# HGRN2's level and state products in a two-layer hybrid encoder: from 128-column products to 64-column blocks on the two halves of the PE array

## The chip, the cores and the metric

One Trainium2 chip; the kernel runs on one of its cores. The metric is device time in microseconds of one execution. An engine executes its own queue in order; TensorE is called PE, VectorE DVE, ScalarE ACT, GpSimdE POOL, the sync engine's queue SP. Weight loads of PE stand under a name of their own, PEld.

## The reference

Two encoder layers over 512 tokens of width 1024. Each layer projects x with one large matrix, feeds three token mixers (HGRN2, dilated attention, latent attention), merges them through gates, projects, and normalizes. The change touches only HGRN2: a gated linear recurrence for 8 heads, key width 128, value width 64, run forward and backward in time:

```
S_t = diag(f_t) S_{t-1} + k_t v_t^T ;  o_t = S_t^T q_t
```

Everything is float32.

## The kernel before

Tokens lie along the free axis, 512 of them in 4 blocks of 128; one tile of 128 partitions holds the 128 key channels of one head. Projections with the large matrices split both operands into a high and a low part and run three passes of single-pass products (lines 291 to 316); they make up most of PE's stream: hq and hf (queries and gates of a head), hv and dv (values), hgg, dl, mg and so on.

`hgrn_levels` (line 686) works for one head as a generator. The recurrence is split in a doubling scheme. In every level m = 1, 2, 4, 8, 16, 32, 64 the running products of gates are folded into qq and kk in place by two DVE multiplications (lines 738, 739). At m = 4 (lines 697 to 721) both directions of the innermost 8-token triangles are made: for each direction, key and query tiles hk and hq are put together from a part that ACT copies (line 707) and a part that POOL multiplies (line 709), four products of 128 x 128 per direction go to PE (line 716), ACT copies the bank to `ha` or `hz` (line 717), POOL clears what lies on the wrong side of the diagonal (line 719), and DVE adds the two (line 721). At m = 8, 16, 32, 64 (lines 722 to 733) ACT gathers the keys kc (line 726), PE makes four products of 128 x 128, one per block of tokens (line 729), and DVE copies under a mask those elements of the product that belong to the level into `ha` (line 733). Each level thus computes all 128 x 128 pairs of a block, and the mask keeps the few that it is for.

After the levels the kk tiles are transposed on PE (line 754), copied by ACT (line 756), and six products of 128 weight columns with 64 moving columns give the block states `hst` (line 762), which DVE chains (lines 766 to 775). `hgrn_pair` (line 779) adds up the outputs of two heads in one bank, the first head on partitions 0 to 63, the second on 64 to 127: products with 64 weight columns, on alternating halves of the array (line 796). `do` (line 975) and `dn` (line 1019) in the dilated attention have that form as well; two of the `do` products per head pair and half move 64 columns only.

Heads go in pairs (lines 1065 to 1075). The two generators of a pair are stepped in turn until both give their result. Then the projections of the next pair are traced (hq, hf) and, for the first two pairs, a value projection of the dilated attention (dv); the first pair's run beside the value projection hv. The engines' queues aren't in the order of tracing: a scheduler at build time, with durations of its own, lays the traced instructions out, earlier-traced first among those it holds ready, so that projections of the next pair lie between the levels of the current one. Buffers bound this: three PSUM banks for such products (`at_bank`), four for projections, 16 tiles of 128 x 512 with tag a2 (hk, hq, kc, ha, hz and others), 6 and 4 large tiles for gates, kk and qq. `after(first, *before)` (line 232) adds a dependency by hand: the instruction `first` waits for those in `before`.

Of the kernel before, what the change touches and what calls it, by code (L numbers as in the profile page):

```python
# [11 lines left out]
I32 = mybir.dt.int32  # L12
# [29 lines left out]

HG_LEVELS = (8, 16, 32, 64)
PI = float(np.pi)


# [14 lines left out]
def host_tables():  # L61

    i = np.arange(128)
    masks = np.zeros((128, len(HG_LEVELS), 128), np.int32)
    for n, m in enumerate(HG_LEVELS):
        a, b = i[:, None], i[None, :]
        masks[:, n, :] = (a // (2 * m) == b // (2 * m)) & (a // m != b // m)
    ident = np.eye(128, dtype=np.float32)
# [129 lines left out]
def tile_encoder(ctx: ExitStack, tc: tile.TileContext, x, xt, positions, blocks, wuq, wuh, par_in, brow, lbp,  # L198
# [40 lines left out]
    con = cst.tile([128, N_CONST], F32, name="con")  # L239
    mask = cst.tile([128, len(HG_LEVELS) * 128], U8, name="mask")  # L240
    ident = con[:, O_ID:O_ID + 128]
# [209 lines left out]
    nc.sync.dma_start(con, consts)  # L451
    mask_i = fap(t4("mask_i", I32), 0, [[1, len(HG_LEVELS) * 128]])
    nc.sync.dma_start(mask_i, masks)
    V.tensor_copy(mask, mask_i)

    def layer(l, x_src, need_next):
# [229 lines left out]
        def hgrn_levels(h, g, v):  # L686
# [9 lines left out]
            while m < 128:  # L696
                if m == 4:

                    rc = fap(f2, 0, [[1, 2 * R]])
                    V.reciprocal(rc, fap(base, 0, [[1, 2 * R]]))  # L700
                    a, z = t2(f"ha{h}_{l}"), t2(f"hz{h}_{l}")
                    for d, dst in ((0, a), (1, z)):
                        kd, qd = t2(f"hk{d}{h}_{l}"), t2(f"hq{d}{h}_{l}")

                        for t, src, plain in ((kd, kk[:, d], m * d), (qd, qq[:, 1 - d], m - m * d)):
                            scaled = m - plain
                            A.copy(fap(t, plain, [[2 * m, R // 2], [1, m]]),  # L707
                                   fap(src, plain, [[2 * m, R // 2], [1, m]]))
                            nc.gpsimd.tensor_tensor(
                                fap(t, scaled, [[2 * m, R // 2], [1, m]]),  # L710
                                fap(src, scaled, [[2 * m, R // 2], [1, m]]),
                                fap(rc, R * (1 - d) + scaled // m, [[2, R // 2], [0, m]]), ALU.mult)
                        sc = at_bank(f"hs{h}_{d}_{l}")
                        for w in range(NT):
                            ws = slice(w * 128, w * 128 + 128)
                            nc.tensor.matmul(sc[:, ws], kd[:, ws], qd[:, ws], start=True, stop=True)  # L716
                        A.copy(dst, sc)  # L717
                        sgn = 1 - 2 * d
                        nc.gpsimd.affine_select(dst, dst, pattern=[[0, NT], [sgn, 128]], compare_op=ALU.is_ge,  # L719
                                                fill=0.0, base=0, channel_multiplier=-sgn)  # L720
                    V.tensor_tensor(a, a, z, ALU.add)
                elif m > 4:

                    sc = at_bank(f"hs{h}_{m}_{l}")
                    kc = t2(f"kc{h}_{m}_{l}")
                    A.copy(fap(kc, 0, [[2 * m, R // 2], [m, 2], [1, m]]),  # L726
                           fap(kk, 0, [[2 * m, R // 2], [S + m, 2], [1, m]]))
                    for w in range(NT):
                        nc.tensor.matmul(sc[:, w * 128:w * 128 + 128], kc[:, w * 128:w * 128 + 128],  # L729
                                         fap(qq, w * 128, [[2 * m, 64 // m], [S + m, 2], [1, m]]),  # L730
                                         start=True, stop=True)
                    n = HG_LEVELS.index(m)
                    ready = [V.copy_predicated(a, bcast(mask[:, n * 128:n * 128 + 128], [[0, 4], [1, 128]]), sc)]  # L733

# [16 lines left out]
            for d, blocks in ((0, (0, 1, 2)), (1, (1, 2, 3))):  # L751
                tr = at_bank(f"hkt{h}{d}_{l}")
                for j, b in enumerate(blocks):
                    nc.tensor.transpose(tr[:, j * 128:j * 128 + 128], kk[:, d, b * 128:b * 128 + 128], ident)  # L754
                kt_ = t2(f"hkt{h}{d}_{l}")
                A.copy(kt_[:, :384], tr[:, :384])  # L756
# [487 lines left out]
```

## Time and profile before

| | us |
|---|---|
| median of 3 runs | 1806.01 (1804.51 to 1806.61) |
| profiled execution | 1804.81 |
| its span in the trace | 1803.1 |
| PE busy in the span | 1776.1 |
| DVE, ACT, POOL busy | 1051.9, 743.5, 569.4 |

The span runs from the first to the last instruction; the execution's own time is 1.7 us more. A busy PE is not PE at its peak, because its records overlap: the time that a group of records takes is read from the start of the first to the start of what follows, not from the sum of durations. A float32 product appears as two MATMUL and two LDWEIGHTS records. In the names of the groups "128*64 128x128" means 128 rows and 64 columns of weights, and 128 partitions by 128 moving columns.

### The profile page before, as it was taken

To read this page: it belongs to the slowest core of one execution; us is meant where nothing else is said; L and a number is where in the kernel's file an instruction comes from. 1 tells how busy PE (TensorE), PEld (TensorE's weight loads), DVE (VectorE), ACT (ScalarE), POOL (GpSimd) and SP (SyncE) were. 2 spreads that over 40 slices of the span, in tenths; PEclk is the share of its full clock that TensorE was granted. 3 is DMA by queue.
4 is the path that set the end of the run, shared out by engine and by line. 5 is a ranking of instruction groups with operands and counts; after the bars stand their busy time and mean duration, and the time that the engine had idled before them with its cause. 6 is when DMAs were issued, how large, how long until landed. Compare 5 with 4: busy or idle time off the path is not lost.

```text
span 1803.1 us, 24561 instructions
## 1 busy us (share of the span) xinstructions
PE 1776.1 (99%) x9656; PEld 1499.6 (83%) x9656; DVE 1051.9 (58%) x1870; ACT 743.5 (41%) x1291; POOL 569.4 (32%) x306
## 2 busy tenths in 40 slices
PE   9999999999999999999999999999999999999987
PEld 7788988988888888887788889889888888888876
DVE  8887766543232466656576767775432324656565
ACT  6545454233334364433254345442424244544330
POOL 0311245134243233333222112542333332433332
PEclk9999999999999999999999999999999999999999
DMA  5212222122222222322242122222222232224222
GB/s 191 89 58 101 70 72 86 59 83 82 71 94 83 68 74 78 119 101 70 94 134 97 62 88 72 70 88 66 64 94 83 71 95 57 90 73 148 76 68 79
DMA packets 77139, 154.10 MB, mean 85 GB/s; under 512 B 37728, under 2 KB 37728, under 8 KB 77024
## 3 DMA queue, kind: packets, MB, share of 16 engines
q1 hardware_dynamic: 77024, 152.54, 26.4%
q8 instruction: 76, 1.25, 0.3%
q14 instruction: 39, 0.32, 0.1%
HBM read 148.22 MB, written 4.29 MB: 85 GB/s over the span
## 4 chain that ended last, share of the span: by engine, by line
PE 93%; DVE 4%; ACT 1%; issue 0%; POOL 0%; DMA 0%; SPq 0%; DVEq 0%
PE mg L297 17%; PE dl L297 15%; PE dv L314 8%; PE hf L297 7%; PE br L297 6%; PE wo L1189 4%; PE hq L297 4%; PE hs L729 3%; PE hgg L297 2%; PE dg L297 2%; PE hv L314 2%; PE st L495 2%; PE cq L297 2%; PE do L975 2%; PE mo L656 2%; PE hs L716 1%
## 5 line engine op out<-in xcount | busy, mean ns | idle before, releaser
L690 POOL TENSOR_TENSOR qq<-hq,fr 128x1024 f32<-128x1024 f32 x16 | 41.9, 2622 | 249.5 <-DVE fr L683 249.5
L739 DVE TENSOR_TENSOR kk<-kk,fr 128x512 f32<-128x512 f32 x96 | 89.1, 946 | 23.6 <-ACT hk L707 16.3
L1035 DVE TENSOR_SCALAR mg<-mg 128x512 f32<-128x512 f32 x32 | 53.6, 1682 | 55.3 <-ACT mg L1034 55.1
L738 DVE TENSOR_TENSOR qq<-qq,fr 128x512 f32<-128x512 f32 x96 | 73.4, 764 | 0.0
L733 DVE COPY_PREDICATED ha<-mask,hs 128x512 f32<-128x512 uint8 x64 | 46.9, 733 | 43.9 <-PE hs L729 43.9
L729 PEld LDWEIGHTS hs<-qq,kc 128*128 128x128 f32 x512 | 62.6, 192 | 2.9 <-ACT kc L726 0.6
L729 PE MATMUL hs<-qq,kc 128*128 128x128 f32 x512 | 63.1, 275 | 0.4 <-DVE qq L738 0.4
L854 DVE CUSTOM_DVE_ANT_0 zb<-dsb,con 128x256 f32<-128x256 f32 x64 | 23.3, 421 | 51.9 <-PE dsb L907 51.9
L726 ACT COPY kc<-kk 128x512 f32<-128x512 f32 x64 | 38.5, 623 | 35.0 <-DVE kk L739 34.9
L756 ACT COPY hkt<-hkt 128x384 f32<-128x384 f32 x32 | 15.0, 507 | 87.7 <-PE hkt L754 87.7
L652 ACT COPY mpt<-mtr 128x128 f32<-128x128 f32 x64 | 17.0, 266 | 77.2 <-DVE mpt L652 77.2
L272 POOL TENSOR_TENSOR wb_0l<-wb_0r,wb_0h 128x1024 fp32r<-128x1024 f32 x12 | 29.3, 2445 | 58.2 <-ACT wb_0h L271 47.2
L272 POOL TENSOR_TENSOR wb_1l<-wb_1r,wb_1h 128x1024 fp32r<-128x1024 f32 x12 | 29.4, 2448 | 56.6 <-ACT wb_1h L271 45.5
L837 DVE TENSOR_SCALAR dl<-dl,par,con 128x512 f32<-128x512 f32 x24 | 25.9, 1080 | 35.1 <-PE dl L297 35.1
L955 ACT ACTIVATE za<-za,dst 128x256 f32<-128x256 f32 x64 | 30.0, 470 | 29.7 <-DVE dst L949 29.7
L652 DVE COPY mpt<-mtr 128x128 f32<-128x128 f32 x64 | 18.5, 288 | 39.9 <-PE mtr L650 32.0
L1035 DVE TENSOR_SCALAR mgc<-mgc 128x512 f32<-128x512 f32 x16 | 24.7, 1546 | 24.3 <-ACT mgc L1034 24.3
L719 POOL TENSOR_SCALAR_AFFINE_SELECT ha<-ha 128x512 f32<-128x512 f32 x16 | 10.3, 645 | 87.5 <-ACT ha L717 61.1
L716 PEld LDWEIGHTS hs<-hq,hk 128*128 128x128 f32 x256 | 33.2, 191 | 4.2 <-issue 2.0
L647 DVE TENSOR_SCALAR mp<-mp,mst 128x512 f32<-128x512 f32 x32 | 35.6, 1111 | 0.9
L716 PE MATMUL hs<-hq,hk 128*128 128x128 f32 x256 | 34.0, 276 | 1.3 <-POOL ha L719 1.3
L656 PE MATMUL mo<-mpt,mv 128*128 128x128 f32 (+1 forms) x192 | 33.5, 309 | 0.0
(1511 smaller groups left out, 5437.8 us busy)
## 6 DMA issues: line engine op xcount, KB each, us to landing
wb_0r<-in_blocks_dram SPq DMA_DIRECT2D x12, 512.0 KB, 3.5
wb_1r<-in_blocks_dram SPq DMA_DIRECT2D x12, 512.0 KB, 3.5
w_0r<-in_blocks_dram SPq DMA_DIRECT2D x9, 512.0 KB, 3.5
w_1r<-in_blocks_dram SPq DMA_DIRECT2D x8, 512.0 KB, 3.5
w_2r<-in_blocks_dram SPq DMA_DIRECT2D x8, 512.0 KB, 3.4
w_3r<-in_blocks_dram SPq DMA_DIRECT2D x8, 512.0 KB, 3.4
wo_0r<-in_blocks_dram SPq DMA_DIRECT2D x8, 512.0 KB, 3.5
wo_1r<-in_blocks_dram SPq DMA_DIRECT2D x8, 512.0 KB, 3.4
```

The source lines that it names most:

```text
L272: (eng or nc.gpsimd).tensor_tensor(lo, raw, hi.bitcast(F32), ALU.subtract)
L297: newest["product"] = nc.tensor.matmul(ps, lhs(a, k), rhs(b, k), start=n == 0, stop=n == 3 * kt - 1)
L314: nc.tensor.matmul(ps, xs[a][2 * j + k][:, toks], w[b][:, k], start=j == 0 and n == 0, stop=j == 3 and n == 5)
L656: nc.tensor.matmul(o[:, cols], v[:, kb, h * 128:h * 128 + 128], pts[kb][:, cols], start=qt == 1 and kb == 0, stop=qt == NT - 1 and kb == N ...
L690: nc.gpsimd.tensor_tensor(qq, bcast(q, [[0, 2], [1, S]]), fr, ALU.mult)
L716: nc.tensor.matmul(sc[:, ws], kd[:, ws], qd[:, ws], start=True, stop=True)
L729: nc.tensor.matmul(sc[:, w * 128:w * 128 + 128], kc[:, w * 128:w * 128 + 128], fap(qq, w * 128, [[2 * m, 64 // m], [S + m, 2], [1, m]]), s ...
L733: ready = [V.copy_predicated(a, bcast(mask[:, n * 128:n * 128 + 128], [[0, 4], [1, 128]]), sc)]
L738: V.tensor_tensor(fap(qq, 0, dims), fap(qq, 0, dims), qf, ALU.mult)
L739: V.tensor_tensor(fap(kk, 0, dims), fap(kk, 0, dims), kf, ALU.mult)
L1035: V.tensor_scalar(g, g, 0.5, 0.5, ALU.mult, ALU.add)
L1189: nc.tensor.matmul(ps, ms[a][2 * kp + k][:, tt * 128:tt * 128 + 128], wo[4 * half + kp][b][k][:, cols], start=(kp, a, b, k) == (0, 0, 0, 0 ...
```

## The change

- The level products at m = 4, 8, 16 and 32 are made for the 64 x 64 blocks on the diagonal only: eight products with 64 weight columns and 64 moving columns, alternately onto partitions 0 to 63 and 64 to 127 of the bank, in place of four of 128 x 128. At m = 64 the eight products are the blocks beside the diagonal.
- At m = 4 both directions share one bank; ACT copies it once (to a new tile `hc`), and four half-width selects on POOL take the place of two.
- Levels 32 and 64 write into one bank, each its own blocks, and share one masked copy after level 64. Levels 8 and 16 have two masked copies, each of 64 partitions and 64 columns of each block.
- The state products go as 64-column halves too: twelve products with 64 weight columns in place of six with 128.
- The generators hand their products out as functions; the loop over pairs calls those of both heads one after the other and makes the first of them wait for the inputs of both heads.
- The table of masks has three entries in place of four.

```diff
-HG_LEVELS = (8, 16, 32, 64)
+HG_MASKS = ((8,), (16,), (32, 64))
+HALVES = [(slice(64 * i, 64 * i + 64), slice(c + 64 * i, c + 64 * i + 64)) for c in range(0, S, 128) for i in range(2)]
...
                     a, z = t2(f"ha{h}_{l}"), t2(f"hz{h}_{l}")
-                    for d, dst in ((0, a), (1, z)):
+                    kds, qds, made = [], [], []
+                    for d in range(2):
                         kd, qd = t2(f"hk{d}{h}_{l}"), t2(f"hq{d}{h}_{l}")
...
-                        sc = at_bank(f"hs{h}_{d}_{l}")
-                        for w in range(NT):
-                            ws = slice(w * 128, w * 128 + 128)
-                            nc.tensor.matmul(sc[:, ws], kd[:, ws], qd[:, ws], start=True, stop=True)
-                        A.copy(dst, sc)
+                    sc, c = at_bank(f"hs{h}_{l}"), t2(f"hc{h}_{l}")
+                    first = None
+                    for d in range(2):
+                        for n, (rows, at) in enumerate(HALVES):
+                            mat = nc.tensor.matmul(sc[rows, 256 * d + 64 * (n // 2):256 * d + 64 * (n // 2) + 64],
+                                                   kds[d][:, at], qds[d][:, at], start=True, stop=True)
+                            first = first or mat
+                    after(first, *made)
+                    A.copy(c, sc)
+
+                    for d, dst in ((0, a), (1, z)):
                         sgn = 1 - 2 * d
-                        nc.gpsimd.affine_select(dst, dst, pattern=[[0, NT], [sgn, 128]], compare_op=ALU.is_ge,
-                                                fill=0.0, base=0, channel_multiplier=-sgn)
+                        for i in range(2):
+                            nc.gpsimd.affine_select(fap(dst, 64 * i, [[128, NT], [1, 64]]),
+                                                    fap(c, 256 * d, [[64, NT], [1, 64]]),
+                                                    pattern=[[0, NT], [sgn, 64]], compare_op=ALU.is_ge, fill=0.0,
+                                                    base=64 * i * sgn, channel_multiplier=-sgn)
                     V.tensor_tensor(a, a, z, ALU.add)
                 elif m > 4:
-                    sc = at_bank(f"hs{h}_{m}_{l}")
+                    if m < 64:
+                        sc = at_bank(f"hs{h}_{m}_{l}")
                     kc = t2(f"kc{h}_{m}_{l}")
...
+                    def products(m=m, sc=sc, kc=kc):
+                        first = None
+                        for n, (rows, at) in enumerate(HALVES):
+                            if m < 64:
+                                to, rhs = at, fap(qq, at.start, [[2 * m, 32 // m], [S + m, 2], [1, m]])
+                            else:
+                                c = at.start + 64 * (1 - 2 * (n % 2))
+                                to = slice(c, c + 64)
+                                rhs = qq[:, 1 - n % 2, to]
+                            mat = nc.tensor.matmul(sc[rows, to], kc[:, at], rhs, start=True, stop=True)
+                            first = first or mat
+                        return first
+
+                    yield [made], products
+                    if m != 32:
+                        n = [m in ms for ms in HG_MASKS].index(True)
+                        for cols in [slice(0, 128)] if m == 64 else [slice(0, 64), slice(64, 128)]:
+                            rows, wd = slice(0, 128) if m == 64 else cols, cols.stop - cols.start
+                            mk = mask[rows, n * 128 + cols.start:n * 128 + cols.stop]
+                            ready = [V.copy_predicated(fap(a[rows], cols.start, [[128, NT], [1, wd]]),
+                                                       bcast(mk, [[0, NT], [1, wd]]),
+                                                       fap(sc[rows], cols.start, [[128, NT], [1, wd]]))]
...
-            yield
-            n = 0
-            for d, blocks in ((0, (0, 1, 2)), (1, (1, 2, 3))):
-                for j, b in enumerate(blocks):
-                    nc.tensor.matmul(st[:, n * 64:n * 64 + 64], kts[d][:, j * 128:j * 128 + 128],
-                                     v[:, b, 64 * h:64 * h + 64], start=n == 0, stop=n == 5, skip_group_check=True)
-                    n += 1
+            def states():
+                first, n = None, 0
+                for d, blocks in ((0, (0, 1, 2)), (1, (1, 2, 3))):
+                    for j, b in enumerate(blocks):
+                        for i in range(2):
+                            c = j * 128 + 64 * i
+                            mat = nc.tensor.matmul(st[64 * i:64 * i + 64, n * 64:n * 64 + 64], kts[d][:, c:c + 64],
+                                                   v[:, b, 64 * h:64 * h + 64], start=n == 0, stop=n == 5,
+                                                   skip_group_check=True)
+                            first = first or mat
+                        n += 1
+                return first
+
+            yield [made], states
...
-            parts = [None]
-            while None in parts:
+            while True:
                 parts = [next(g) for g in both]
+                if parts[0] is None:
+                    continue
+                if len(parts[0]) > 2:
+                    break
+
+                firsts = [go() for _, go in parts]
+                after(firsts[0], *parts[0][0], *parts[1][0])
```

At level 4 the wait is for the inputs of the head itself (`after(first, *made)`), at the later levels and the states for those of both heads.

## Rows read from the trace of the kernel before

**Rows 1.** The page: busy time, share of the span and instructions of each engine; PE's granted clock in 40 slices, in tenths of full speed; the chain that ended last by engine.

```profile
PE 1776.1 (99%) x9656; PEld 1499.6 (83%) x9656; DVE 1051.9 (58%) x1870; ACT 743.5 (41%) x1291; POOL 569.4 (32%) x306
...
PEclk9999999999999999999999999999999999999999
...
PE 93%; DVE 4%; ACT 1%; issue 0%; POOL 0%; DMA 0%; SPq 0%; DVEq 0%
```

**Rows 2.** Busy time by stage, from the first pair's level products in layer 0 on: stretch and its length, then busy us (and records) of PE, PEld, DVE, ACT and POOL, granted clock, DMA share and GB/s.

```profile
62.00:92.00 30.00, 27.28 (x135) 22.68 (x134) 21.04 (x28) 23.95 (x35) 7.69 (x9) 1.00 0.30 100
...
138.00:211.00 73.00, 73.00 (x412) 66.53 (x411) 55.24 (x84) 33.85 (x54) 14.76 (x14) 1.00 0.23 76
```

**Rows 3.** What PE waited for over the whole run: who waited for whom, us in total, times, longest us.

```profile
PE hq L297 <- DVE hv L511: 1.4, 1, 1.4
...
PE hs L716 <- POOL ha L719: 1.3, 1, 1.3
...
PE hs L729 <- DVE qq L738: 0.4, 1, 0.4
```

**Rows 4.** Groups of PE instructions by line and shape: busy us and mean ns of one, then idle time before them.

```profile
L729 PE MATMUL hs<-qq,kc 128*128 128x128 f32 x512 | 63.1, 275 | 0.4 <-DVE qq L738 0.4
L716 PE MATMUL hs<-hq,hk 128*128 128x128 f32 x256 | 34.0, 276 | 1.3 <-POOL ha L719 1.3
L762 PE MATMUL hst<-hv,hkt 128*128 128x64 f32 x192 | 23.7, 276 | 0.0
```

**Rows 5.** PE in order of time: start and duration in us, then line, operation, names, shape and count. Level products inside the projection stream, second pair of layer 0.

```profile
163.28 1.98 PE L297 MATMUL hf<-xh,w_1664h 128*128 128x512 f32 x8
165.09 1.95 PE L729 MATMUL hs<-qq,kc 128*128 128x128 f32 x16
166.79 2.07 PE L297 MATMUL hf<-xl,w_1664h 128*128 128x512 f32 x8
168.71 1.98 PE L297 MATMUL hf<-xh,w_1664l 128*128 128x512 f32 x8
170.52 1.98 PE L297 MATMUL hf<-xh,w_2688h 128*128 128x512 f32 x8
...
180.11 1.95 PE L729 MATMUL hs<-qq,kc 128*128 128x128 f32 x16
```

**Rows 6.** The same view where the dilated attention's products run on the two halves of the array, 64 weight columns and 128 moving columns, between two stretches of the stream.

```profile
656.84 0.39 PE L609 MATMUL mvps<-mvw0l,ckvn 128*128 128x512 f32 x1
657.16 1.09 PE L975 MATMUL do<-dtb30p,dv 128*64 128x128 f32 x16
658.08 1.04 PE L975 MATMUL do<-dtb31p,dv 128*64 128x128 f32 x16
658.95 1.04 PE L1019 MATMUL dn<-con,dden 128*64 128x128 f32 x16
659.93 0.50 PE L609 MATMUL mvps<-mvw0l,ckvn 128*128 128x512 f32 x1
660.26 0.86 PE L609 MATMUL mvps<-mvw0h,ckvn 128*128 128x512 f32 x3
```

**Rows 7.** The same view at a place where the last 8 records of such a run move 64 columns (the shape printed for a merged group is that of its first record).

```profile
434.79 1.09 PE L975 MATMUL do<-dta00p,dv 128*64 128x128 f32 x16
435.71 0.84 PE L975 MATMUL do<-dta01p,dv 128*64 128x128 f32 x16
436.48 0.66 PE L986 MATMUL dtb<-con,zb 128*128 128x128 f32 x4
```

**Rows 8.** The instructions of that line: durations in ns as minimum, median and maximum, first and last start, and the shapes, both layers together.

```profile
L975 PE MATMUL do<-dta01p,dv x32: 219/248/273, 435.7 to 1330.3; 128*64 128x128 f32 x16, 128*64 128x64 f32 x16
```

**Rows 9.** PE in order of time around the output products of a pair: 40 records on the halves between 203.06 and 205.39.

```profile
202.50 0.63 PE L314 MATMUL dv<-w_2l,xh 128*128 128x512 f32 x2
203.06 0.44 PE L796 MATMUL ho<-ha,hv 128*64 128x128 f32 x4
...
205.39 0.87 PE L314 MATMUL dv<-w_3h,xh 128*128 128x512 f32 x2
206.10 0.40 PE L314 MATMUL dv<-w_3h,xl 128*128 128x512 f32 x1
```

**Rows 10.** POOL in order of time at the level-4 stage of the third pair; in brackets its idle time before, and what ended it.

```profile
201.41 1.13 POOL L709 TENSOR_TENSOR hq<-qq,f 128x256 f32<-128x256 f32 x1
...
213.61 0.67 POOL L709 TENSOR_TENSOR hk<-kk,f 128x256 f32<-128x256 f32 x1
...
219.58 0.64 POOL L719 TENSOR_SCALAR_AFFINE_SELECT hz<-hz 128x512 f32<-128x512 f32 x1 [4.67 <-ACT hz L717]
220.19 0.67 POOL L709 TENSOR_TENSOR hk<-kk,f 128x256 f32<-128x256 f32 x1
220.81 1.12 POOL L709 TENSOR_TENSOR hq<-qq,f 128x256 f32<-128x256 f32 x1
```

**Rows 11.** DVE in order of time after the level run that began at 173.24.

```profile
175.79 0.73 DVE L733 COPY_PREDICATED ha<-mask,hs 128x512 f32<-128x512 uint8 x1
176.41 0.68 DVE L738 TENSOR_TENSOR qq<-qq,fr 128x512 f32<-128x512 f32 x1
```

**Rows 12.** Groups of instructions by line: DVE's masked copies and POOL's selects.

```profile
L733 DVE COPY_PREDICATED ha<-mask,hs 128x512 f32<-128x512 uint8 x64 | 46.9, 733 | 43.9 <-PE hs L729 43.9
...
L719 POOL TENSOR_SCALAR_AFFINE_SELECT ha<-ha 128x512 f32<-128x512 f32 x16 | 10.3, 645 | 87.5 <-ACT ha L717 61.1
```

More of the change, by code (lines that the diff above doesn't have):

```diff
@@ L63, in host_tables @@
     i = np.arange(128)
-    masks = np.zeros((128, len(HG_LEVELS), 128), np.int32)
-    for n, m in enumerate(HG_LEVELS):
+    masks = np.zeros((128, len(HG_MASKS), 128), np.int32)
+    for n, ms in enumerate(HG_MASKS):
         a, b = i[:, None], i[None, :]
-        masks[:, n, :] = (a // (2 * m) == b // (2 * m)) & (a // m != b // m)
+        for m in ms:
+            masks[:, n, :] |= (a // (2 * m) == b // (2 * m)) & (a // m != b // m)
     ident = np.eye(128, dtype=np.float32)
@@ L239, in tile_encoder @@
     con = cst.tile([128, N_CONST], F32, name="con")
-    mask = cst.tile([128, len(HG_LEVELS) * 128], U8, name="mask")
+    mask = cst.tile([128, len(HG_MASKS) * 128], U8, name="mask")
     ident = con[:, O_ID:O_ID + 128]
@@ L451, in tile_encoder @@
     nc.sync.dma_start(con, consts)
-    mask_i = fap(t4("mask_i", I32), 0, [[1, len(HG_LEVELS) * 128]])
+    mask_i = fap(t4("mask_i", I32), 0, [[1, len(HG_MASKS) * 128]])
     nc.sync.dma_start(mask_i, masks)
@@ L706, in hgrn_levels @@
                             scaled = m - plain
-                            A.copy(fap(t, plain, [[2 * m, R // 2], [1, m]]),
-                                   fap(src, plain, [[2 * m, R // 2], [1, m]]))
-                            nc.gpsimd.tensor_tensor(
+                            made.append(A.copy(fap(t, plain, [[2 * m, R // 2], [1, m]]),
+                                               fap(src, plain, [[2 * m, R // 2], [1, m]])))
+                            made.append(nc.gpsimd.tensor_tensor(
@@ L717, in hgrn_levels @@
-                        A.copy(dst, sc)
-                        sgn = 1 - 2 * d
-                        nc.gpsimd.affine_select(dst, dst, pattern=[[0, NT], [sgn, 128]], compare_op=ALU.is_ge,
-                                                fill=0.0, base=0, channel_multiplier=-sgn)
+                                fap(rc, R * (1 - d) + scaled // m, [[2, R // 2], [0, m]]), ALU.mult))
+                        kds.append(kd)
+                        qds.append(qd)
+                    sc, c = at_bank(f"hs{h}_{l}"), t2(f"hc{h}_{l}")
@@ L721, in hgrn_levels @@
                     V.tensor_tensor(a, a, z, ALU.add)
                 elif m > 4:
-                    sc = at_bank(f"hs{h}_{m}_{l}")
+                    if m < 64:
+                        sc = at_bank(f"hs{h}_{m}_{l}")
                     kc = t2(f"kc{h}_{m}_{l}")
[L726 to L731, printed above, removed]
@@ L732, in hgrn_levels @@
-                    n = HG_LEVELS.index(m)
-                    ready = [V.copy_predicated(a, bcast(mask[:, n * 128:n * 128 + 128], [[0, 4], [1, 128]]), sc)]
+                    made = A.copy(fap(kc, 0, [[2 * m, R // 2], [m, 2], [1, m]]),
+                                  fap(kk, 0, [[2 * m, R // 2], [S + m, 2], [1, m]]))
+                    def products(m=m, sc=sc, kc=kc):
[10 more added lines that the diff above has]
+                        return first
@@ L755, in hgrn_levels @@
                 kt_ = t2(f"hkt{h}{d}_{l}")
-                A.copy(kt_[:, :384], tr[:, :384])
+                made = A.copy(kt_[:, :384], tr[:, :384])
                 kts.append(kt_)
-            yield
-            n = 0
-            for d, blocks in ((0, (0, 1, 2)), (1, (1, 2, 3))):
-                for j, b in enumerate(blocks):
-                    nc.tensor.matmul(st[:, n * 64:n * 64 + 64], kts[d][:, j * 128:j * 128 + 128],
-                                     v[:, b, 64 * h:64 * h + 64], start=n == 0, stop=n == 5, skip_group_check=True)
-                    n += 1
+            def states():
[11 more added lines that the diff above has]
+            yield [made], states
             s = t2(f"hS{h}_{l}")
```

1 line of the change is left out of this document (removed).

## The prediction

> **What bounds the kernel now.** First the page's busy times and its chain of waits: PE is busy 1776 of 1803 us, 93% of the chain that ended last is PE, and the granted clock is full in every slice [rows 1]. Then the table of stages: over one whole head pair, 138 to 211 us, PE is busy all 73.00 us, while DVE has 55 and POOL 15 [rows 2]. Then what PE waited for: the three largest waits that the HGRN2 code causes are 1.4, 1.3 and 0.4 us in the whole run [rows 3]. So TensorE is the limit around the change, and what shortens its stream shortens the kernel, as long as the inputs of the shortened runs come in time.
>
> **Products, before.** A float32 product is two records. The change touches 512 + 256 + 192 = 960 of them [rows 4]. From 163.28 to 168.71 us lie 16 records of the projection stream and one run of 16 level products [rows 5]. The stream steps by (170.52 - 168.71)/8 = 0.226 us a record, so 5.43 - 16 x 0.226 = 1.81 us belong to the 16 products: 0.113 each, entering and leaving included. The state products move only 64 columns, yet their busy time per record, 23.7/192, equals the levels' 63.1/512 [rows 4]: with 128 columns of weights, half the moving columns buy nothing. All 960 get 0.113: 108.5 us.
>
> **Products, after.** Each record becomes two, with 64 weight columns and 64 moving columns, on alternating halves: 960 pairs. The kernel already has such pairs. With 128 moving columns, the 16 records from 658.08 to 658.95 us step through in 0.87 us, 0.109 per pair [rows 6]. With 64 moving columns there is one place: the last 8 of the 16 records of dta01p [rows 7, 8]. From 435.71 to the transposes at 436.48 are 0.77 us; 4 pairs of the wide form take 0.436, which leaves 0.334 for 4 narrow pairs and for leaving the mode. If leaving cost nothing a pair would be 0.084, the upper end. Leaving cost 0.98 - 0.87 = 0.11 us at 659.93 [rows 6], which gives 0.056. The durations say the same: 219 ns narrow against 273 wide [rows 8], 54 less, so 0.109 - 0.054 = 0.055, the lower end. I take 0.057: 54.7 us.
>
> The Trainium skill ("TensorEngine Tiling (Array Packing)", Performance Considerations, Instruction Overhead) speaks against this: each matmul carries some 60 cycles, and no factor should be taken from a dimension that is small already. As an estimate, 60 cycles at the granted clock, 25 ns, on top of 0.057 would make 0.082 a pair and 78.7 us. The last rows show less than that as soon as any cost of leaving is taken off, so I stay at 0.057 and keep the upper end as rival (e).
>
> **Switching between the forms.** From 656.84 to 660.26 us lie 24 wide pairs and two stream records [rows 6]: 3.42 - 24 x 0.109 - 2 x 0.227 = 0.35 us is for going into the halves and back. From 202.50 to 206.10 us, with 20 pairs and four stream records [rows 9], it is 3.60 - 2.18 - 0.91 = 0.51. The runs after: at level 4 one per head, since only there each head's products wait for that head alone; at levels 8, 16, 32, 64 and the states one for both heads together: 7 x 8 pairs = 56. At 0.35 that is 19.6 us, at 0.51 28.6; I take 0.40, since the smaller value was measured on the longer stretch: 22.4 us. It holds only if the heads stay together.
>
> **Waits added.** The first product of a run now waits for all inputs of the run. PE works in order, so behind it stands the whole projection stream, and behind that the ACT and DVE reads of its banks. At levels 8 to 64 nothing new appears: the runs already have 16 records, both heads. After one such run DVE was through at 176.41 + 0.68 = 177.09 and the next run began at 180.11 [rows 5, 11]: 3.0 us of slack, against 0.5 us that a run gets shorter (1.81 to 16 x 0.057 + 0.40). At level 4 four runs become two, each behind four ACT copies and four POOL products. POOL's were 0.67 to 1.13 us each, but half of them stood behind a select that itself waited for ACT's copy of the run before, 4.67 us of POOL idleness at 219.58 [rows 10]; this waiting goes away. What covers the collection is the projection stream of the next pair. If that cover is gone, four POOL products at 1.1 us show on PE for each head. One place has thin cover: the first pair of layer 0, where PE was already idle 2.7 of 30 us [rows 2]. There I write off 2 us. At the states the first head no longer covers the second head's last copy, about 0.15 us a pair: 1 us.
>
> **The rest, off the path.** Level 32 loses its masked copy, levels 8 and 16 do two half ones: per head 4 x 0.733 becomes between 0.73 + 4 x 0.37 = 2.2 and 0.73 + 4 x 0.73 = 3.7 us, on a DVE with 18 us free per pair [rows 2, 12]. The nearer end is the low one, since half the columns are read. Four half selects on POOL replace two of 0.65: 1.3 to 2.6 us per head, covered by POOL's 58 idle us per pair. ACT saves one copy per head. Two PSUM banks per pair serve longer (32 and 64 share), two fewer are used at level 4. The eight hk/hq tiles of a pair are alive together and the previous pair's four tiles have to be free; its output run stood ahead of level 4 already. One mask less is loaded. All of it at nothing, hidden under the projections; uncovered it would be 1 to 2 us per pair.
>
> **Sum.** 108.5 - 54.7 - 22.4 - 3 = 28.4 us less, against the profiled execution's 1804.8: 1776.4. The runs' median stands 1.2 us above that execution, so 1777.6; the rivals' times are on the same footing.
>
> **Rivals.**
> (a) The narrow price does not hold in long runs. It was seen on 4 pairs; runs now have 16 to 24. If two products can't be issued faster than the 0.109 us that long runs show [rows 6], 960 pairs cost 104.6 and the switches 22.4: 127 against 108.5, 18.5 us slower with no stall, 1824 us. The halves not running together at all comes out alike. It decides where a pair costs over (108.5 - 25.4)/960 = 0.087 us. For it: no long narrow run exists. Against it: the wide price equals what 128 columns of weights cost, 0.113, so it looks like work and not issue, and it fell with the columns. The Trainium skill ("TensorE: Matmul & The Clock Gate", Wait — 56ns, not 53.3ns?) names a sequencer cost near 62 ns per matmul in one decoding mode; as an estimate 0.124 a pair, 119 us, 1839 in all. Rows 6 step at 0.054 per record over 32 records, which is under it, so that mode is not in force here.
> (b) The waits eat most: level 4 waits some 3 us in each of 8 pairs for POOL and ACT, 24 us: 1802. For it: POOL products took up to 1.13 us beside DVE [rows 10]. Against it: PE waited 1.3 us in all for that line so far [rows 3].
> (c) The order of the queues is worked out at build by a scheduler with its own durations; if it parts the heads, 96 switches cost 38.4: 1794. Against it: the heads' runs of 16 are joined without being made to.
> (d) Other engines set the pace of a pair and PE merely idles more: within 0.2% of 1806. Against it: 18 us of DVE slack in 73.
> (e) A narrow pair costs the upper end, 0.084: 80.6 us, and 108.5 - 80.6 - 22.4 - 3 = 2.5 us less, 1803.5. For it: the 0.334 us are measured as a whole, the share of leaving comes from another place. Against it: the durations, 54 ns shorter [rows 8]. The skill's 60 cycles, above, would end close to here.
>
> **How the numbers follow.** Forecast 0.70; (a) 0.07; (b) 0.11; (c) 0.05; (d) 0.04; (e) 0.03. About 0.2% (3.6 us) is what a measurement can tell from no change. Faster takes the forecast, (b) and (c): 0.86; same (d) and (e): 0.07; slower (a): 0.07. The low end: pairs at 0.055, switches at 0.35, no stall: 108.5 - 52.8 - 19.6 = 36 us, 1770; a few us for waits that close up elsewhere: 1765. The high end: pairs at 0.058, switches at 0.51 and 8 us of waits leave 108.5 - 55.7 - 28.6 - 8 = 16 us, 1790; to hold (c) and the milder half of (b) it goes to 1796.
>
> **What would show it.** Narrow level products as 64-column records, two starting within some 10 ns and pairs 0.055 to 0.060 us apart; runs of 32 and 48 records; PE's span over a pair near 69.5 us instead of 73, with PE still busy throughout. The forecast is wrong if the runs step at 0.1 us per pair, if they come singly per head, or if PE's waits for level-4 inputs grow from 1.3 us to tens.

## The result and the profile after

| | before | after |
|---|---|---|
| median (4 runs each) | 1805.39 us | 1780.70 us (1779.61 to 1782.48) |
| ratio | | 0.9863, 95% interval 0.9851 to 0.9875 |
| profiled execution | 1804.81 | 1780.54 |
| its span | 1803.1 | 1778.8 |

The kernel became 24.7 us faster, 1.37%; 28.4 us had been forecast. The kernel before has one run more in this table than ahead of the prediction, hence its other median. The two spans differ by 24.3 us, and the accounts below are made on them.

The page of the kernel after answers to [rows 1]:

```profile
PE 1745.7 (98%) x10616; PEld 1451.2 (82%) x10616; DVE 1048.8 (59%) x1886; ACT 731.7 (41%) x1273; POOL 574.6 (32%) x338
```

PE is still the bound, with 960 MATMUL records more and 30.4 us less of busy time. (The chain that ended last can be followed back only to 537 us here; 61 of its 70 hundredths of the span are PE, against 93 of 100 before.) The stages answer to [rows 2]; the third line is one stretch inside the first. Columns: stretch and length, busy us and records of PE, PEld, DVE, ACT, POOL, granted clock, DMA share, GB/s.

```profile
62.00:92.00 30.00, 26.84 (x191) 21.82 (x192) 24.88 (x40) 20.01 (x32) 8.51 (x12) 0.94 0.31 91
137.00:205.50 68.50, 68.50 (x536) 60.24 (x532) 55.47 (x92) 33.56 (x53) 15.32 (x18) 1.00 0.28 88
67.53:70.94 3.41, 3.41 (x10) 2.63 (x9) 3.41 (x7) 0.75 (x3) 3.41 (x6) 0.50 0.04 14
```

A whole pair of heads keeps PE busy throughout, as before. From the first pair's output products to the second pair's it now takes 68.6 us in place of 73.1. The first pair of layer 0 is different: the granted clock is 0.94 there, because 3.4 us of it ran at 0.50, the lower of the two levels.

PE in order of time around a level run of layer 0's second pair, then around its state run, and around the end of that pair and the start of the next pair's level 4; these answer to [rows 5, 9]. Columns: start and duration in us, line, operation, names, shape, count.

```profile
154.16 1.07 PE L300 MATMUL hf<-xh,w_2560l 128*128 128x512 f32 x4
155.16 1.15 PE L754 MATMUL hs<-qq,kc 128*64 128x64 f32 x32
156.24 1.19 PE L300 MATMUL hf<-xh,w_2560l 128*128 128x512 f32 x4
157.27 1.08 PE L300 MATMUL hq<-xh,w_640h 128*128 128x512 f32 x4
...
185.62 0.63 PE L317 MATMUL dv<-w_2l,xh 128*128 128x512 f32 x2
186.18 1.62 PE L798 MATMUL hst<-hv,hkt 128*64 128x64 f32 x48
187.73 0.86 PE L317 MATMUL dv<-w_0h,xh 128*128 128x512 f32 x2
188.43 0.64 PE L317 MATMUL dv<-w_0h,xl 128*128 128x512 f32 x2
...
205.58 0.39 PE L837 MATMUL ho<-qq,hS 128*64 128x128 f32 x4
205.80 1.10 PE L723 MATMUL hs<-hq,hk 128*64 128x64 f32 x32
```

Here is the reading. Eight stream records lie between 154.16 and 157.27, so 3.11 - 8 x 0.227 = 1.295 us belong to 32 narrow records, entering and leaving included; the same work cost 1.81 before. Inside a run two records start 6 to 7 ns apart and the next two 58 ns after the first two: 16 x 0.058 = 0.93, and 0.37 is left for the two switches. The 48 state records take 188.43 - 185.62 - 4 x 0.227 = 1.90 us here (1.76 to 1.91 over the runs); before, 24 records took 2.70. At 205.80 the level-4 run of the next pair's first head follows the output products with no stream record between: both are in the halves form, and the two share their switches.

What PE waited for (us, times, longest), against [rows 3]:

```profile
PE hs L754 <- DVE qq L771: 5.6, 7, 1.0
...
PE hq L300 <- DVE hv L514: 3.2, 1, 3.2
```

The groups of products by shape, against [rows 4]:

```profile
L754 PE MATMUL hs<-qq,kc 128*64 128x64 f32 x1024 | 38.2, 225 | 5.6 <-DVE qq L771 5.6
L723 PE MATMUL hs<-hq,hk 128*64 128x64 f32 x512 | 18.6, 224 | 0.0
L798 PE MATMUL hst<-hv,hkt 128*64 128x64 f32 x384 | 12.9, 224 | 0.0
```

Waits for level 4 are nil. Waits at the levels behind it went from 0.4 us to 5.6, and the wait in the first pair from 1.4 to 3.2.

### The profile page after: what moved, and what is told of

It is laid out like the page before. It is cut to its first block, busy times and chain, and to the rows that moved or that the text cites. A ratio compares the mean times of both kernels' runs of the same rounds, so it can differ in the third digit from the quotient of the medians.

```text
span 1778.8 us, 26441 instructions
## 1 busy us (share of the span) xinstructions
PE 1745.7 (98%) x10616; PEld 1451.2 (82%) x10616; DVE 1048.8 (59%) x1886; ACT 731.7 (41%) x1273; POOL 574.6 (32%) x338
## 4 chain that ended last, share of the span: by engine, by line
PE 61%; DVE 4%; ACT 2%; DMA 1%; issue 1%; POOL 1%; SPq 0%; DVEq 0%; ACTq 0%
PE mg L300 14%; PE dl L300 6%; PE br L300 5%; PE wo L1236 5%; PE hf L300 4%; PE dv L317 4%; PE cq L300 2%; PE hq L300 2%; PE mo L659 2%; PE ckv L300 1%; PE hgg L300 1%; PE hv L317 1%; PE do L1016 1%; PE st L498 1%; PE qn L300 1%; PE dg L300 1%
## 5 line engine op out<-in xcount | busy, mean ns | idle before, releaser
L772 DVE TENSOR_TENSOR kk<-kk,fr 128x512 f32<-128x512 f32 x96 | 93.4, 992 | 32.8 <-ACT kc L742 21.7
L771 DVE TENSOR_TENSOR qq<-qq,fr 128x512 f32<-128x512 f32 x96 | 75.3, 797 | 17.0 <-POOL qq L693 15.2
L764 DVE COPY_PREDICATED ha<-mask,hs 64x256 f32<-64x256 uint8 (+1 forms) x80 | 40.4, 505 | 16.7 <-PE hs L754 15.5
L754 PEld LDWEIGHTS hs<-qq,kc 128*64 128x64 f32 x1024 | 33.3, 137 | 17.6 <-issue 8.8
L732 POOL TENSOR_SCALAR_AFFINE_SELECT ha<-hc 128x256 f32<-128x256 f32 x32 | 12.8, 424 | 105.0 <-ACT hc L727 104.8
L754 PE MATMUL hs<-qq,kc 128*64 128x64 f32 x1024 | 38.2, 225 | 5.6 <-DVE qq L771 5.6
L713 POOL TENSOR_TENSOR hk<-kk,f 128x256 f32<-128x256 f32 x32 | 23.8, 745 | 51.5 <-DVE fr L775 51.5
L789 ACT COPY hkt<-hkt 128x384 f32<-128x384 f32 x32 | 15.4, 480 | 60.3 <-PE hkt L787 59.9
L1201 DVE SCALAR_TENSOR_TENSOR res<-res,wo 128x256 f32<-128x256 f32 x32 | 12.1, 416 | 38.1 <-PE wo L1236 38.0
L659 PE MATMUL mo<-mpt,mv 128*128 128x128 f32 (+1 forms) x192 | 33.5, 309 | 0.0
```

Source lines behind the costliest of these rows:

```text
L659: nc.tensor.matmul(o[:, cols], v[:, kb, h * 128:h * 128 + 128], pts[kb][:, cols], start=qt == 1 and kb == 0, stop=qt == NT - 1 and kb == N ...
L754: mat = nc.tensor.matmul(sc[rows, to], kc[:, at], rhs, start=True, stop=True)
L764: ready = [V.copy_predicated(fap(a[rows], cols.start, [[128, NT], [1, wd]]), bcast(mk, [[0, NT], [1, wd]]), fap(sc[rows], cols.start, [[12 ...
L771: V.tensor_tensor(fap(qq, 0, dims), fap(qq, 0, dims), qf, ALU.mult)
L772: V.tensor_tensor(fap(kk, 0, dims), fap(kk, 0, dims), kf, ALU.mult)
```

## The experiments

All ratios are against runs of the kernel before on the same chip, with 95% intervals. Where a run is set against the change in us, two medians are subtracted that weren't measured side by side; by the ratios most of these distances are smaller, by up to 1.7 us. Diffs are against the kernel after unless said otherwise.

**Which part of the new form is cheap: the smaller block, or the two halves at once?** e2 keeps the products and gives each head's products of one half first, then those of the other.

```diff
-                        for n, (rows, at) in enumerate(HALVES):
+                        for n, (rows, at) in sorted(enumerate(HALVES), key=lambda t: t[0] % 2):
...
             def states():
-                first, n = None, 0
-                for d, blocks in ((0, (0, 1, 2)), (1, (1, 2, 3))):
-                    for j, b in enumerate(blocks):
-                        for i in range(2):
+                first = None
+                for i in range(2):
+                    n = 0
+                    for d, blocks in ((0, (0, 1, 2)), (1, (1, 2, 3))):
+                        for j, b in enumerate(blocks):
...
```

> The changed kernel with the same narrow products, but all of one half of the array before all of the other, so that neighbours share a half. Theory 1 (the gain is that the two halves run at the same time): each narrow record takes its 0.055 to 0.058 us alone, 960 x 0.055 = 53 us more than the change: 1834 us, slower than before; a level run of 32 records lasts 1.9 us or more. Rival (narrow records are simply short, the overlap brings nothing): as the change, 1781 us.

Measured: 1803.44 us, ratio 0.9984 [0.9974, 0.9994], between the two. PE around the same run as above:

```profile
156.85 1.07 PE L300 MATMUL hf<-xh,w_2560l 128*128 128x512 f32 x4
157.85 1.54 PE L754 MATMUL hs<-qq,kc 128*64 128x64 f32 x32
159.32 1.20 PE L300 MATMUL hf<-xh,w_2560l 128*128 128x512 f32 x4
160.35 0.85 PE L300 MATMUL hq<-xh,w_640h 128*128 128x512 f32 x3
```

3.50 - 8 x 0.227 = 1.69 us in place of 1.295. Records on the same half start 58 ns apart, and wherever the order changes to the other half some three pairs of records start 4 to 6 ns apart. With three changes of half in a run the overlap was not gone. So I formed a theory: a record costs 58 ns by itself, and each change hides three. e12 has one change per run, both heads' first halves and then both heads' second ones (at level 4, where a run belongs to one head, that head's).

```diff
-                firsts = [go() for _, go in parts]
+                firsts = [go(half) for half in range(2) for _, go in parts]
...
+                            if n % 2 != half:
+                                continue
...
```

> As e2, but one half of the array gets all its products of a run (both heads) before the other half gets any: each run changes halves once, where e2 changed three times and the change at every product. Theory 1 (a narrow record takes 0.058 us on its own half, and only some three records on each side of a change of halves overlap): a run of 32 takes 0.37 + 29 x 0.058 = 2.05 us in place of 1.29 (e2: 1.69), a state run 3.05 in place of 1.84; 46 us more than the change, 1826 us, slower than before. Rival (neighbours on one half overlap too, some 0.042 us a record as e2's mean has it): as e2, 1803 us.

Measured: 1824.47 us, ratio 1.0103 [1.0086, 1.0119]. The same view:

```profile
160.41 1.52 PE L300 MATMUL hf<-xh,w_2560l 128*128 128x512 f32 x6
161.86 1.90 PE L757 MATMUL hs<-qq,kc 128*64 128x64 f32 x32
163.69 0.73 PE L300 MATMUL hf<-xh,w_2560l 128*128 128x512 f32 x2
164.25 1.09 PE L300 MATMUL hq<-xh,w_640h 128*128 128x512 f32 x4
```

3.84 - 8 x 0.227 = 2.02 us (2.05 over the runs), as (32 - 3) x 0.058 + 0.37 = 2.05 says; state runs took 3.05. The theory holds. The same products, with the same blocks, become 18 us slower than the kernel before when the halves take turns: two records of 58 ns cost as much as one wide record (0.113 us), and the switches come on top. Without the overlap nothing of the gain is left.

**The parts.** e3 puts back the wide state products.

```diff
-                        for i in range(2):
-                            c = j * 128 + 64 * i
-                            mat = nc.tensor.matmul(st[64 * i:64 * i + 64, n * 64:n * 64 + 64], kts[d][:, c:c + 64],
...
+                        mat = nc.tensor.matmul(st[:, n * 64:n * 64 + 64], kts[d][:, j * 128:j * 128 + 128],
...
```

> The changed kernel with the state products 128 columns wide again, still both heads in one run. Theory 1 (0.058 us a pair and 0.37 to 0.45 us of switching per run): a state run costs 24 x 0.113 = 2.71 us in place of 1.84, 8 runs: 7 us more, 1787.6 us. Rival (the states' part is bought back by what waits behind them): within 2 us of the change.

Measured: 1786.26 us, ratio 0.9891 [0.9877, 0.9904], 5.6 us more than the change. A joint run of 24 wide records took 2.77 us, so the runs alone say (2.77 - 1.85) x 8 = 7.4 us. The executions spread over 3.8 us, so the part is worth what its runs say as nearly as can be told.

e4 puts back level 4 as it was: wide products, a bank per direction, full selects, no added wait. The later levels stay changed.

```diff
-                    sc, c = at_bank(f"hs{h}_{l}"), t2(f"hc{h}_{l}")
...
-                    after(first, *made)
-                    A.copy(c, sc)
...
+                        sc = at_bank(f"hs{h}_{d}_{l}")
+                        for w in range(NT):
+                            ws = slice(w * 128, w * 128 + 128)
+                            nc.tensor.matmul(sc[:, ws], kd[:, ws], qd[:, ws], start=True, stop=True)
+                        A.copy(dst, sc)
```

> The changed kernel with level 4 as before: two banks, two copies, two selects, eight products of 128 columns per head. Theory 1: four runs of 0.905 us per pair in place of 1.295 us and 0.79 us (the first head's run mostly follows the pair's output products in the same form, 3.49 against 2.70 us): 12 us more, 1793 us; up to 4 us of it may come back if the pause and the lower clock in the first pair go away. Rival (level 4's fewer, later runs cost what they save): within 2 us of the change.

Measured: 1807.03 us, ratio 1.0003 [0.9994, 1.0012]: 26 us more than the change, where 12 had been expected and the rival had said 2 at most. The level-4 runs cost what was expected, 4 x 0.905 us per pair; the rest is in waits that the kernel after doesn't have in this size: PE's idle time is 36.1 us against 23.2, and these 12.9 us with the runs' 12 are about the 24.6 by which the spans differ. PE's waits, then two lines of its order of time:

```profile
PE hst L786 <- ACT hkt L777: 7.1, 4, 1.8
PE hs L742 <- DVE qq L759: 6.3, 3, 2.4
```

```profile
246.05 0.69 PE L742 MATMUL hs<-qq,kc 128*64 128x64 f32 x16
249.11 0.69 PE L742 MATMUL hs<-qq,kc 128*64 128x64 f32 x16 [2.38 <-DVE qq L759]
```

PE stands 2.38 us in the middle of a run, because the scheduler's queues put the second head's `qq` late, and the state run stands 1.8 us for a copy four times. The edit changes level 4's banks, its runs and its waits at once, and the whole queue is laid out differently; which of the three brings these waits isn't shown.

**The joint order.** e1 is the kernel before, its wide products and all else, with only the order of the change: both heads' products in one run, the first waiting for the inputs of both.

```diff
-                    for w in range(NT):
-                        nc.tensor.matmul(sc[:, w * 128:w * 128 + 128], kc[:, w * 128:w * 128 + 128],
...
+                    def products(m=m, sc=sc, kc=kc):
...
+                    yield [made], products
...
-            parts = [None]
-            while None in parts:
+            while True:
                 parts = [next(g) for g in both]
```

> The joint order of the change (both heads' level products at m = 8 to 64 and both heads' states in one run, the first product waiting for both heads' inputs), with every product 128 columns wide as before; masks, level 4 and copies as before. Theory 1 (the narrow halves are the whole gain): as before, 1805 us, give or take 3; level runs step at 0.112 us per record. Rival (the joint order itself frees time): 1780 to 1795 us.

Measured: 1834.73 us, ratio 1.0156 [1.0143, 1.0170]. Both expectations were missed: with wide products the joint order costs 29 us. PE's largest wait, one line of its order of time, and the stretch that follows, with the columns of [rows 2]:

```profile
PE hst L769 <- ACT hkt L763: 7.3, 4, 1.8
```

```profile
197.08 5.11 PE L769 MATMUL hst<-hv,hkt 128*128 128x64 f32 x24 [1.83 <-ACT hkt L763]
```

```profile
197.40:204.20 6.80, 6.80 (x28) 6.38 (x28) 3.79 (x10) 3.41 (x6) 2.37 (x1) 0.50 0.01 4
```

The state run stands 1.83 us for the last copy, and behind that stop PE runs 6.8 us at half the clock. Five such stretches, 27 us in sum, lie in the HGRN2 stages, where the kernel before has none; PE is busy throughout them, so they cost about half of that, some 13 us. PE's idle time in pauses of over 0.48 us grew from 14.7 to 29.3 us. The level runs themselves cost what they did, 0.1124 us a record. So the order brings a kernel with wide products nothing.

e5 is the reverse: narrow products, but each head's are traced by itself, as before the change.

```diff
-                    yield [made], products
+                    products()
...
-                firsts = [go() for _, go in parts]
-                after(firsts[0], *parts[0][0], *parts[1][0])
```

> The changed kernel without the joint wait: each head issues its level and state products when its own inputs are there, in the order that the build lays out (level runs stay joined in it, the states of a pair fall into three runs). Theory 1 (a run costs some 0.37 us for the switch, and the joint wait itself costs nothing): 16 more runs, 6 us more, 1786.6 us. Rival (the joint wait costs PE time, the 5.6 us that PE now waits for DVE at the levels): as fast as the change or faster, 1775 to 1781 us.

Measured: 1788.74 us, ratio 0.9898 [0.9884, 0.9912], 8 us more than the change. The scheduler still joined the level runs; the states fell into three runs per pair, and two pairs of eight, not six, had their level-4 run merged with output products. PE's waits for `qq` are 4.9 us, about as many as with the added wait (5.6), so the added wait itself costs next to nothing. Sixteen more runs and four lost merges of some 0.5 us each make 16 x 0.37 + 2 = 7.9 us. So for narrow products the joint order is worth these 6 (by the ratios) to 8 us, in switches saved; it is a part of the 24.7.

e8 joins level 4's two heads too: one run of 64 records per pair.

```diff
-                    after(first, *made)
...
+                    yield made, products4
```

> The changed kernel with the level-4 products of both heads in one run of 64 records, the first waiting for both heads' keys and queries. Theory 1 (a run costs a switch of 0.37 us): 8 runs fewer, 3 us less, 1778 us. Rival (the longer collection shows as PE waits at level 4): 2 to 10 us more than the change, with PE waits on POOL or ACT at that line.

Measured: 1793.44 us, ratio 0.9926 [0.9913, 0.9939], 12.7 us more than the change: the rival. PE's waits, then one such run in order of time:

```profile
PE hs L758 <- DVE qq L775: 8.7, 4, 2.3
PE hs L725 <- POOL hq L713: 6.5, 3, 2.9
```

```profile
269.30 2.08 PE L725 MATMUL hs<-hq,hk 128*64 128x64 f32 x64 [1.83 <-POOL hq L713]
```

A clean run of 64 took 2.24 us, so 16 more pairs cost 2.24 - 1.295 = 0.945, 0.059 each: the narrow price holds in long runs. The saved switches (8 x 0.37 = 3 us) are lost again, since none of the eight level-4 runs follows the output products directly any more, where six did (6 x 0.5 us). What is left is waiting: PE is idle for 33.5 us in place of 23.2, for POOL's products of both heads and for `qq`.

**The first pair.** In the kernel after PE stands 3.16 us behind the first pair's level-4 run in layer 0, waiting for DVE to empty the banks of `hv`; in the same stage DVE computes the rotary tables for the dilated attention. e6 traces these tables later, behind the four pairs; e7 does the same to the kernel before; e9, e10 and e11 trace them inside the dilated attention, behind the scores and the merge of its head pair 0, 1 and 2.

```diff
         hv = in_tm(C_HI, "hv")
-        if l == 0:
-            shared["rope"] = rope_tables()
...
         ya = hgrn_out(os_, hg)
+        if l == 0:
+            shared["rope"] = rope_tables()
```

> The changed kernel with the rotary tables (some 40 DVE instructions, made once) built after the HGRN2 heads of layer 0 in place of beside the first pair. Theory 1 (PE's pause of 3.4 us after the first pair's first run, and the lower clock that follows, come from DVE being full there): the pause and the drop go, 4 to 5 us less, 1776 us. Rival (the pause has another cause, or the tables delay something as much where they go): 1780 us or more.

Measured: 1787.01 us, ratio 0.9889 [0.9874, 0.9903], 6 us more than the change. The pause and its half clock went (first line, columns as in [rows 2]), and the first pair's output products began 7.5 us earlier, so DVE's work on the tables is what made the pause. Then PE stood still further on (second line):

```profile
62.00:92.00 30.00, 30.00 (x239) 24.44 (x239) 23.47 (x30) 17.98 (x29) 10.43 (x13) 1.00 0.30 97
395.00:410.00 15.00, 5.76 (x19) 4.33 (x19) 2.35 (x2) 14.82 (x25) 4.75 (x2) 0.66 0.12 35
```

PE and ACT in order of time there:

```profile
404.68 3.48 PE L300 MATMUL mg<-xh,w_10560h 128*128 128x512 f32 x8 [9.24 <-ACT w_10560h L274]
```

```profile
397.43 1.28 ACT L376 ACT_TABLE_LOAD   x1
398.72 0.63 ACT L376 ACTIVATE sin<-r_r 128x512 f32<-128x512 f32 x1
...
403.07 0.63 ACT L379 ACTIVATE cos<-r_u 128x512 f32<-128x512 f32 x1
403.60 1.03 ACT L274 CAST w_10560h<-w_10560r 128x1024 fp32r<-128x1024 f32 x1
```

PE's next weights need a cast by ACT, and in ACT's queue this cast stands behind the tables' sine and cosine, each behind a table load of 1.28 us, with a third such load between them.

e7 makes the same edit on the kernel before.

> The kernel before with the rotary tables built at the same later place. Theory 1: only its two shorter pauses of 1.5 us each go, 2 to 3 us less, 1802.6 us; so the tables cost the changed kernel more than the kernel before. Rival: as much less as in the changed kernel (4 to 5 us), or no less.

Measured: 1807.85 us, ratio 1.0012 [1.0003, 1.0021]: no gain there either, with new PE waits of 1.3 us at 384 and 3.5 us at 413, the second for the same cast.

e9, e10 and e11 (`hp == 0`, `1`, `2`):

```diff
+            if hp == 0 and l == 0:
+                shared["rope"] = rope_tables()
...
```

> The changed kernel with the rotary tables built after the first pair's scores and first merge of the dilated attention, later than in the run before it (e6), so that more of the attention's own DVE work stands ahead of them. Theory 1 (the first pair loses 5 us or more to the tables, which DVE could make in its idle time later): the pauses of 9.6 and 2.8 us that e6 had at 368 to 405 us shrink, 1772 to 1777 us. Rival (wherever they stand, 20 us of DVE work in one piece stops PE as long): 1781 to 1788 us.

> The same one pair of the dilated attention later. Theory 1: 1772 to 1777 us. Rival: 1781 to 1788 us.

> The same one pair later again, just ahead of the latent attention's inputs that use the tables. Theory 1: 1772 to 1777 us, if the tables are still ready in time. Rival: 1781 us or more, with PE waiting for the rotary key.

Measured: 1783.02 (0.9879 [0.9864, 0.9894]), 1792.43 (0.9929 [0.9917, 0.9941]) and 1788.27 us (0.9901 [0.9887, 0.9914]).

Theory 1 failed in all three: e9 and e11 end in the rival's range, e11 without the wait for the rotary key that it named, and e10 4 us above it. At each place PE has long waits for DVE that the kernel after has not (e9 7.2 us for `dta00p`, e10 9.2 for `acc` and 5.4 for `dta10p`, e11 11.7 for `dta20p`). No version beat the change; e9's interval overlaps that of the change, the others cost more than the first pair does.

## Why the prediction was right

**The narrow price** was right: 0.058 us a pair against 0.057, in runs of 32, 48 and 64. The Trainium skill ("TensorEngine Tiling (Array Packing)", Performance Considerations, Instruction Overhead) spoke of some 60 cycles for each matmul, which as an estimate made 0.082 a pair. The runs disagree: a pair with 128 moving columns takes 0.109 [rows 6] and one with 64 takes 0.058, so, if the cost is linear between these two, 64 columns cost 0.051 and 0.007 is left for all that doesn't depend on them. Rival (e) falls.

**Rival (a)**, no overlap in long runs, 1824 us, did not come about in this order of products. e12 shows that its price was right: 1824.5 us is what the same blocks cost with the halves one after the other.

**The switches** were right: 0.37 per level run against 0.40, and 0.37 to 0.51 around the states. Of the 56 runs that were counted, six level-4 runs merge with the output products before them (3.49 us together in place of 2.70 + 1.295, 0.5 saved each): 3 us that the prediction didn't count. It leaned to the smaller of its two values for being measured on the longer stretch, which holds in pairs (24 against 20) and not in time (3.42 us against 3.60).

**At level 4** PE waits for no input, against rival (b)'s 24 us. But e4 and e8 show how close it lies: with another layout of level 4 the waits eat some half of the gain. The 1 us that the sum sets aside at the states was worked out from no row, and the kernel after doesn't show it: PE never waits at `hst` there (idle 0.0 in its group); with e4's layout it waits 7.1 us at that place.

**"At levels 8 to 64 nothing new appears"** was the step that failed. The 3.0 us of slack [rows 5, 11] were taken at one run of one pair; over all pairs the waits for `qq` grew from 0.4 to 5.6 us, 5.2 us for which the sum had nothing. (The list of HGRN2's waits in the prediction also leaves out 0.5 us of `hkt` for ACT, twice 0.2; nothing hangs on it.) The added wait names the copies of kc alone, and the `qq` of the second head may still be late: then PE stands inside the run, as here in the third pair.

```profile
237.09 0.69 PE L754 MATMUL hs<-qq,kc 128*64 128x64 f32 x16
...
238.73 0.69 PE L754 MATMUL hs<-qq,kc 128*64 128x64 f32 x16 [0.96 <-DVE qq L771]
```

The merged runs made up for it. At the measured prices a pair's runs take 6 x 1.295 - 0.375 + 1.85 = 9.25 us in place of 108.5/8 = 13.56: 4.3 us less, and 4.5 was measured on the pair at 137.00, which has no such wait. Less (5.6 - 0.4)/8 = 0.65 for the waits it is 3.7; the sum gave 3.9. That two things left out, waits and merges, nearly cancel is luck.

**The stages.** By the same products in both traces (the group `cqms` behind HGRN2's stage in each layer, first and last start), before and then after:

```profile
L531 PE MATMUL cqms<-con,cqq x16: 250/251/272, 618.3 to 1513.0; 128*128 128x1 f32 x16
```

```profile
L534 PE MATMUL cqms<-con,cqq x16: 250/250/271, 606.0 to 1487.7; 128*128 128x1 f32 x16
```

Layer 0 gained 12.3 us up to there; the start of layer 1's level products is 959.63 - 949.69 = 9.9 us early; layer 1's mark is 25.3 early, so its stage gained 15.4; the end is 24.3 early. The sum, by layers, was 15.7 less 0.5 for the states: 15.2 for layer 1, and 13.2 for layer 0 with the 2 us for its first pair. So layer 1 came out as predicted, 3.85 a pair, layer 0 was 0.9 us short, and 12.3 - 9.9 + 25.3 - 24.3 = 3.4 us were lost where no part of the change is. These 3.4 us are nearly all of the difference between forecast and result; the prediction had no term for them.

**The first pair.** PE in order of time, before and after:

```profile
61.67 1.05 PE L716 MATMUL hs<-hq,hk 128*128 128x128 f32 x8
64.14 2.09 PE L297 MATMUL hq<-xh,w_256h 128*128 128x512 f32 x8 [1.42 <-DVE hv L511]
```

```profile
61.91 1.15 PE L723 MATMUL hs<-hq,hk 128*64 128x64 f32 x32
66.22 2.64 PE L300 MATMUL hq<-xh,w_256h 128*128 128x512 f32 x8 [3.16 <-DVE hv L514]
```

The 2 us written off for it are about right by luck, since the cause is another. It isn't level 4's inputs: before, PE stood 1.42 us for DVE and 1.3 for POOL [rows 3], after, 3.16 for DVE alone, since the stream record behind the run needs a bank that DVE, busy without a gap from 62 to 66 us, empties late. PE's idle time in the stage grew only from 2.72 to 3.16 us. But behind the one longer pause the clock is granted at 0.50 for 3.4 us: steps of 0.427 us in place of 0.227, so that 8 records lose 1.6 us. With the 0.44 us of idle time that makes the 2.

**Between the layers** the kernel after has another such stretch, and the kernel before has not, though PE waits there as long in both. Before, then after: `wo` in order of time around the pause, then the stretch behind it.

```profile
856.78 0.39 PE L1189 MATMUL wo<-wo,mm30h 128*128 128x512 f32 x1
859.84 0.74 PE L1189 MATMUL wo<-wo,mmh 128*128 128x512 f32 x2 [2.66 <-ACT wo L1144]
...
859.80:863.20 3.40, 3.02 (x12) 2.19 (x13) 0.00 (x0) 1.14 (x2) 3.16 (x2) 1.00 0.27 108
```

```profile
844.66 0.39 PE L1236 MATMUL wo<-wo,mm30h 128*128 128x512 f32 x1
847.69 0.73 PE L1236 MATMUL wo<-wo,mmh 128*128 128x512 f32 x2 [2.64 <-ACT wo L1191]
...
849.18:852.59 3.41, 3.41 (x9) 2.27 (x8) 0.00 (x0) 1.14 (x2) 3.39 (x3) 0.50 0.40 118
1729.82:1733.23 3.41, 3.41 (x9) 2.46 (x8) 0.00 (x0) 1.13 (x2) 3.41 (x3) 0.50 0.33 77
```

The lead of the kernel after falls from 856.78 - 844.66 = 12.1 us to 863.79 - 852.76 = 11.0 over this stretch (starts of the same `wo` records). A third stretch of this kind, at 1729.82 (last line), lies behind the same pause in layer 1, where the kernel before again has none, and there 1.0 us is lost to the end. So 2.1 of the 3.4 us are found. Of the other 1.3, 0.2 go before the pause (12.3 at `cqms`, 12.1 at `wo`) and 1.1 between 852.76 and layer 1's first level products; of these, 0.7 stand ahead of the last transposes of layer 1's input (`xps`), where PE was idle for 1.07 us before and for 1.76 after, and the profile names nothing that it waits for. Why the same pause, 2.66 and 2.64 us, brings the lower clock in one kernel and not in the other stays open.

**The rest off the path** was right: half masked copies took 446 ns each and the joint one 740, so 4 x 0.446 + 0.74 = 2.5 us per head (2.2 to 3.7 predicted); POOL's half selects 424 and 663 ns, 2.2 us per head (1.3 to 2.6).

## What to carry to other kernels

Products with 64 columns of weights paid here only when neighbours in PE's queue lay on different halves: alternate product by product, price a pair by a run of the same form in the trace, and charge each run its 0.4 us of switching. When PE is the bound and the layout of the queues comes from a scheduler, a shorter run moves the waits: measure each part put back by itself, since here the new order cost 29 us with wide products and saved 6 to 8 with narrow ones, and one level's old form cost the whole gain. Slack read at one run does not hold for all of them; read it at the worst one.

## What the runs showed that I had not expected

- Records on the same half step by 58 ns, and only some three pairs overlap where the order passes to the other half. One change of half per run gave 2.02 us, three gave 1.69, alternation gave 1.295, for the same 32 records.
- A pause of PE can cost more than its length: 3.4 us (in e1 6.8 us) at half the granted clock behind it. Equal pauses of 2.6 us went with and without it.
